# Second feed-forward sub-layer: VectorE transposes SwiGLU's result in 32x32 blocks instead of TensorE

## The chip, the cores and the metric

The kernel runs as one program on one core of a Trainium2 chip. The metric is the device time of one execution in microseconds (us): 1877.92 us, the median of three runs (1877.18 to 1877.95). The engines are named as in the profile: PE is TensorE (matmul), PEld its weight load, DVE is VectorE, ACT is ScalarE, POOL is GpSimd, and SP issues the transfers from HBM.

## What is computed

One decoder layer on 256 tokens of width 2048: a feed-forward sub-layer, a mixer, and a second feed-forward sub-layer (index 1). The change touches only the second feed-forward. Cut to what matters:

```
D_MODEL, SEQ, D_FF = 2048, 256, 5632

def swiglu(h, w_gate, w_up, w_down):
    return (jax.nn.silu(h @ w_gate) * (h @ w_up)) @ w_down

x = sublayer(x, 0, ffn(0), 0.5)
x = sublayer(x, 1, mixer, 1.0)
x = sublayer(x, 2, ffn(1), 0.5)     # sublayer: sandwich RMSNorm with adaLN shift, scale and gate
```

## The kernel before, in words

All data is float32. Each product is made of three matmuls in the fp32r type: a weight is split into a high part `wh` and a rest `wl`, the activations into `hh` and `hl`, and `mm3` (lines 308 to 311) adds high by high (L309), high activation by weight rest (L310) and activation rest by high weight (L311). The high part is a copy on ACT (L290, `wh`), the rest a subtraction on DVE (L291, `wl`).

Weights arrive as tiles `raw` of 128 x 1024 numbers (two blocks of 128 rows by 512 columns, 512 KB), in a ring of eight. Their split parts stand in rings of four buffers each (`NW = 4`, pool `wsp`). So the split of a tile waits until PE is done with the tile four places earlier. A tile takes twelve matmuls: two row blocks, two groups of 128 tokens, three products. Here "tile 0" is the first weight tile of a block's gate product.

The feed-forward's 5632 columns are taken in 11 blocks of 512. A block has eight tiles of the gate weights and eight of the up weights; both products stand in four PSUM banks with the tokens on the partitions (`proj_tok`). Then `swiglu_evac` takes the block out of PSUM: for each group `t` of 128 tokens ACT makes silu of the gate (L522) and DVE multiplies it with the up product (L523), which gives `gt`, 128 tokens x 512 columns. The product with `w_ff_down` wants the columns on the partitions, so `to_g` transposes each 128 x 128 piece on PE against an identity (L513: four into one PSUM bank, two banks a block), and `split_act` (L343 to L345) copies the high part of each bank into the slot `g` on ACT (L344) and subtracts on DVE (L345).

The blocks are taken in three groups of 4, 4 and 3. After a group the down product runs over four column quarters, with the same weight tiles and rings. A block's `g` is wanted only when the down product reaches its rows.

The order: `swiglu_evac` and `to_g` are generators in the list `pending`. After each weight tile's matmuls `pump` advances the first of them by one step, so a block's evacuation is issued among the first tiles of what comes next. A scheduler then orders each engine's instructions by its own costs; each engine runs its list strictly in order. A side job, `ada_unit`, works on the adaLN gate of the last sub-layer in between: DVE accumulates into `acc` from 16 transfers of `w_ada` (L168, L170), in a pool `adap` of two buffers with the tag `acc`, and `ada_row` finishes it (L200, L205 to L207).

Of the kernel before, what the change touches and what calls it, by code (L numbers as in the profile page):

```python
# [8 lines left out]
F32 = mybir.dt.float32  # L9
# [5 lines left out]
P = 128  # L15
D = 2048
S = 256
NT = S // P
# [14 lines left out]
def tile_layer(  # L33
# [6 lines left out]
    nc = tc.nc  # L40
    x, out, c = x[0], out[0], c[0]
# [15 lines left out]
    adap = ctx.enter_context(tc.tile_pool(name="adap", bufs=2))  # L57
# [7 lines left out]
    def nm(s):  # L65
        uid[0] += 1
        return f"{s}_{uid[0]}"

    def ps():
        return psp.tile([P, 512], F32, tag="ps", name=nm("ps"))  # L70

    def t2(shape=(P, 512), dtype=F32):
        return tp.tile(list(shape), dtype, tag="t2", name=nm("t2"))
# [178 lines left out]
    pending = []  # L252
# [17 lines left out]
    def flush():  # L270
        while pending:
            pump()
# [35 lines left out]
    def mm3(o, lh, ll, rh, rl, start, stop):  # L308
        nc.tensor.matmul(o, lh, rh, start=start, stop=False, skip_group_check=True)  # L309
        nc.tensor.matmul(o, lh, rl, start=False, stop=False, skip_group_check=True)  # L310
        nc.tensor.matmul(o, ll, rh, start=False, stop=stop, skip_group_check=True)  # L311
# [20 lines left out]
    def proj_tok(src, c0, begun=None, w=512, segs=FULL, banks=None, first=0):  # L332

        if begun is not None:
            banks, segs = begun[0], FULL[begun[1]:]
        banks = banks or [ps(), ps()]
        last = segs[-1][0] + segs[-1][1] - 1
        for k, wh, wl in w_tiles(src, segs, c0, w=w):
            for t in range(NT):
                tok_mm(k, wh, wl, t, banks[t][:, 0:w], first, last)  # L340
        return banks

    def split_act(dh, dl, src):  # L343
        act = nc.scalar.copy(dh, src)  # L344
        return nc.vector.tensor_tensor(out=dl, in0=src, in1=dh.bitcast(F32), op=ALU.subtract), act  # L345


    def parts():

        p = small((P, 8), "parts")  # L350
        nc.gpsimd.memset(p[:, 3:4], EPS)
        return p

    def sumsq(p, q, src):
        junk = t2()
        nc.scalar.activation(junk, src, AF.Square, scale=float(D) ** -0.5, accum_out=p[:, q + q // 3:q + q // 3 + 1])
# [81 lines left out]
    def early_w(src, c0, w):  # L438


        if src is None:
            return None
        tiles = []
        for half, h in enumerate((hh, hl)):
            raw = load_w(src, 2 * half, c0, w)
            v = h[:, 8:16, :].rearrange("p (a j u) s -> p a j (u s)", a=2, j=2)
            wh, wl = split_w(raw[:, :, 0:w], v, w)
            tiles += [(2 * half + j, wh[:, j, :], wl[:, j, :]) for j in range(2)]
        return tiles
# [54 lines left out]
        return banks, 2  # L504


    def to_g(g, gts):
        for i in range(2):
            pg = ps()
            for j in range(2):  # L510
                for t in range(NT):
                    m = 2 * i + j
                    nc.tensor.transpose(pg[:, j * S + t * P:j * S + (t + 1) * P], gts[t][:, m * P:(m + 1) * P], ident)  # L513
            split_act(g.t[:, 0, 2 * i:2 * i + 2, :], g.t[:, 1, 2 * i:2 * i + 2, :],
                      pg.rearrange("p (k s) -> p k s", s=S))
            yield

    def swiglu_evac(g, gb, ub):
        gts = []
        for t in range(NT):  # L520
            sg, gt = t2(), t2()
            nc.scalar.activation(sg, gb[t], AF.Silu)  # L522
            nc.vector.tensor_tensor(out=gt, in0=sg, in1=ub[t], op=ALU.mult)  # L523
            gts.append(gt)
        yield
        yield
        yield from to_g(g, gts)

    def swiglu_sum(gb, ub, part):

        pv = part.t.rearrange("p k s -> p (k s)")
        gts = []
        for t in range(NT):
            sg, gt = t2(), t2()
            nc.vector.tensor_tensor(out=sg, in0=pv[:, t * 512:(t + 1) * 512], in1=gb[t], op=ALU.add)
            nc.scalar.activation(sg, sg, AF.Silu)
            nc.vector.tensor_tensor(out=gt, in0=pv[:, 1024 + t * 512:1024 + (t + 1) * 512], in1=ub[t], op=ALU.add)
            nc.vector.tensor_tensor(out=gt, in0=sg, in1=gt, op=ALU.mult)
            gts.append(gt)
        part.free()  # L540
        g = Slot((P, 2, 4, S), F32R)

        def rest():
            yield
            yield
            yield from to_g(g, gts)

        pending.append(rest())
        return g

    def ffn(idx, supers, begun, xin, nxt, nxt_src=None, nxt_c0=None, nxt_w=512):

        y = None
        yp = [parts() for _ in range(NT)]

        def evac_y(si, q, t, bank):
            ys = y[t].t[:, q * 512:(q + 1) * 512]
            if si == 0:
                nc.scalar.copy(ys, bank)
            else:  # L560
                nc.vector.tensor_tensor(out=ys, in0=ys, in1=bank, op=ALU.add)
            if si == len(supers) - 1:
                sumsq(yp[t], q, ys)

        for si, blocks in enumerate(supers):
            gs = []
            n = len(blocks)
            for b, segs, part, banks in blocks:
                if si == 0 and begun is not None and not gs:
                    gb = proj_tok(w_ff_gate[idx], b * FB, begun)  # L570
                    ub = proj_tok(w_ff_up[idx], b * FB)
                elif part is not None:
                    gb = proj_tok(w_ff_gate[idx], b * FB, segs=segs, first=segs[0][0])
                    ub = proj_tok(w_ff_up[idx], b * FB, segs=segs, first=segs[0][0])
                    flush()
                    gs.append(swiglu_sum(gb, ub, part))
                    continue
                else:
                    gb = proj_tok(w_ff_gate[idx], b * FB, segs=segs, banks=banks and banks[0])
                    ub = proj_tok(w_ff_up[idx], b * FB, segs=segs, banks=banks and banks[1])  # L580
                flush()
                gs.append(Slot((P, 2, 4, S), F32R))
                pending.append(swiglu_evac(gs[-1], gb, ub))
            if y is None:
                y = [Slot((P, D)) for _ in range(NT)] if xin[0].__class__ is Half else [Half(t) for t in range(NT)]
            rows = [(4 * i, 4, 4 * b[0]) for i, b in enumerate(blocks)]

            def mms(k, wh, wl, t):
                g = gs[k // 4].t
                mm3(banks[t], g[:, 0, k % 4, t * P:(t + 1) * P], g[:, 1, k % 4, t * P:(t + 1) * P],  # L590
                    wh, wl, k == 0, k == 4 * n - 1)

            for q in range(4):
                banks = [ps(), ps()]
                if si == len(supers) - 1 and q == 2:
                    for s_ in xin:
                        s_.t
                if si == len(supers) - 1 and q == 3:
                    flush()
                    if side[0] is not None:  # L600
                        side[0].drain()
                    early = early_w(nxt_src, nxt_c0, nxt_w)
                    kept, slots = hold(w_ff_down[idx], rows, q * 512, NW if nxt is None else 3)

                    def last_mm(t):
                        for k, wh, wl in kept:
                            mms(k, wh, wl, t)

                    return boundary(last_mm, lambda t: evac_y(si, q, t, banks[t]), lambda t: times_gg(y, t, q), xin, y, yp, slots + gs,
                                    early, 1, nxt, nxt_src, nxt_c0, nxt_w)  # L610
                else:
                    for k, wh, wl in w_tiles(w_ff_down[idx], rows, q * 512):
                        for t in range(NT):
                            mms(k, wh, wl, t)
                    for t in range(NT):
                        later(evac_y, si, q, t, banks[t])
                        if si == len(supers) - 1:
                            later(times_gg, y, t, q)
            if si < len(supers) - 1:
                for g in gs:  # L620
                    g.free()
# [102 lines left out]

    blocks = [(4718, 410), (4308, 410), (3896, 412), (3484, 412), (G0, 412)]
    begun = ffn(0, supers, None, xin, 1, w_in, *blocks[0])
    side[0] = None

# [384 lines left out]
```

## Time and profile before

| what | value |
|---|---|
| median of three runs | 1877.92 us |
| the profiled execution, its own time | 1877.58 us |
| its span | 1875.9 us |
| PE busy | 1827.3 us, 97% |
| DVE busy | 1355.3 us, 72% |
| ACT busy | 853.4 us, 45% |
| TensorE clock, mean granted | 0.998 |

Busy times overlap between engines. The second feed-forward lies between about 1130 us and the end. A timeline row gives start, duration, engine, line, operation, output<-input and count; in brackets stands the idle time before it and what ended it. On one engine the start of the next instruction comes before the recorded end of the one ahead, since the records overlap a little; the distance from start to start is what an instruction costs in a row of them.

### The profile page before, as it was taken

To read this page: it belongs to the slowest core of one execution; us is meant where nothing else is said; L and a number is where in the kernel's file an instruction comes from. 1 tells how busy PE (TensorE), PEld (TensorE's weight loads), DVE (VectorE), ACT (ScalarE), POOL (GpSimd) and SP (SyncE) were. 2 spreads that over 40 slices of the span, in tenths; PEclk is the share of its full clock that TensorE was granted. 3 is DMA by queue.
4 is the path that set the end of the run, shared out by engine and by line. 5 is a ranking of instruction groups with operands and counts; after the bars stand their busy time and mean duration, and the time that the engine had idled before them with its cause. 6 is when DMAs were issued, how large, how long until landed. Compare 5 with 4: busy or idle time off the path is not lost.

```text
span 1875.9 us, 23017 instructions
## 1 busy us (share of the span) xinstructions
PE 1827.3 (97%) x8493; PEld 1530.3 (82%) x8493; DVE 1355.3 (72%) x1472; ACT 853.4 (45%) x1059; POOL 17.2 (1%) x40
## 2 busy tenths in 40 slices
PE   2999999999999999999999999999999999999998
PEld 2888888888888888799988887888888888888886
DVE  7788798788887878868898987555556555556555
ACT  3545444444443444555545446444444444334443
POOL 0000000000000000000000000000000000000000
PEclk9999999999999999999999999999999999999999
DMA  9999889999899999678789994776677776677652
GB/s 349 344 362 351 294 294 311 319 316 310 291 334 327 323 330 315 199 230 276 225 280 309 365 334 138 224 221 213 227 226 218 225 221 216 221 227 222 190 189 93
DMA packets 232618, 499.82 MB, mean 266 GB/s; under 512 B 16829, under 2 KB 28333, under 8 KB 231993
## 3 DMA queue, kind: packets, MB, share of 16 engines
q1 hardware_dynamic: 232504, 498.36, 79.9%
q8 instruction: 66, 1.08, 0.2%
q14 instruction: 48, 0.39, 0.1%
HBM read 496.19 MB, written 2.10 MB: 266 GB/s over the span
## 4 chain that ended last, share of the span: by engine, by line
PE 88%; issue 8%; DVE 2%; ACT 1%; POOL 1%; DMA 0%; SPq 0%; DVEq 0%; POOLq 0%; ACTq 0%
PE ps L309 29%; PE ps L311 28%; PE ps L310 28%; DVE acc L170 1%; PE ps L513 1%; PE ps L181 0%; DMA t<-in_g_pre_dram 0%; PE ps L411 0%; POOL rstd L362 0%; DVE wl L291 0%; ACT t L373 0%; PE ps L900 0%; POOL brs L778 0%; ACT hh L344 0%; PE ps L205 0%
## 5 line engine op out<-in xcount | busy, mean ns | idle before, releaser
L291 DVE TENSOR_TENSOR wl<-raw,wh 128x1024 fp32r<-128x1024 f32 (+2 forms) x637 | 768.6, 1210 | 457.5 <-ACT wh L290 456.9
L290 ACT CAST wh<-raw 128x1024 fp32r<-128x1024 f32 (+2 forms) x637 | 662.4, 1043 | 863.1 <-PE ps L311 737.5
L309 PE MATMUL ps<-wh,hh 128*128 128x512 f32 (+2 forms) x1680 | 651.6, 390 | 3.8 <-DVE t L386 2.4
L310 PE MATMUL ps<-wl,hh 128*128 128x512 f32 (+2 forms) x1680 | 648.6, 386 | 0.6 <-DVE wl L291 0.6
L311 PE MATMUL ps<-wh,hl 128*128 128x512 f32 (+2 forms) x1680 | 648.7, 386 | 0.0
L309 PEld LDWEIGHTS ps<-wh,hh 128*128 128x128 f32 x1680 | 315.8, 188 | 63.5 <-ACT hh L344 4.1
L310 PEld LDWEIGHTS ps<-wl,hh 128*128 128x128 f32 x1680 | 316.2, 188 | 61.2 <-DVE wl L291 2.6
L311 PEld LDWEIGHTS ps<-wh,hl 128*128 128x128 f32 x1680 | 315.6, 188 | 60.5
L170 DVE SCALAR_TENSOR_TENSOR acc<-raw,cs,acc 128x1024 f32<-128x1024 f32 x270 | 345.1, 1278 | 0.5
L309 PE MATMUL ps<-wh,big 128*128 128x512 f32 x804 | 315.4, 392 | 0.0
L311 PE MATMUL ps<-wh,big 128*128 128x512 f32 x804 | 313.2, 390 | 0.0
L310 PE MATMUL ps<-wl,big 128*128 128x512 f32 x804 | 312.8, 389 | 0.0
L311 PEld LDWEIGHTS ps<-wh,big 128*128 128x128 f32 x804 | 150.9, 188 | 31.9
L310 PEld LDWEIGHTS ps<-wl,big 128*128 128x128 f32 x804 | 151.0, 188 | 30.5
L309 PEld LDWEIGHTS ps<-wh,big 128*128 128x128 f32 x804 | 151.0, 188 | 30.5
L650 ACT COPY big<-ps 128x512 f32<-128x512 f32 x32 | 18.9, 589 | 44.2 <-PE ps L311 43.1
L309 PE MATMUL ps<-hh,wh 128*128 128x256 f32 x128 | 37.6, 294 | 0.0
L345 DVE TENSOR_TENSOR big<-ps,big 128x512 fp32r<-128x512 f32 x52 | 35.6, 684 | 1.2 <-ACT big L344 1.2
L311 PE MATMUL ps<-hh,wl 128*128 128x256 f32 x128 | 36.2, 283 | 0.0
L310 PE MATMUL ps<-hl,wh 128*128 128x256 f32 x128 | 36.2, 283 | 0.0
L181 PE MATMUL ps<-ident,acc 128*128 128x128 f32 x96 | 14.5, 285 | 18.6 <-DVE acc L170 18.6
L344 ACT CAST big<-ps 128x512 fp32r<-128x512 f32 x52 | 30.1, 578 | 0.0
(191 smaller groups left out, 756.9 us busy)
## 6 DMA issues: line engine op xcount, KB each, us to landing
raw<-in_w_ada_dram SPq DMA_DIRECT2D x224, 512.0 KB, 5.3
raw<-in_w_ff_gate_dram SPq DMA_DIRECT2D x176, 512.0 KB, 4.5
raw<-in_w_ff_up_dram SPq DMA_DIRECT2D x176, 512.0 KB, 4.6
raw<-in_w_ff_down_dram SPq DMA_DIRECT2D x176, 512.0 KB, 4.9
raw<-in_w_ada_dram SPq DMA_DIRECT2D x128, 256.0 KB, 5.4
raw<-in_w_in_dram SPq DMA_DIRECT2D x48, 512.0 KB, 5.0
raw<-in_w_out_dram SPq DMA_DIRECT2D x32, 512.0 KB, 7.0
raw<-in_w_in_dram SPq DMA_DIRECT2D x24, 412.0 KB, 4.4
```

The lines of the kernel that those rows point to most:

```text
L170: ins = nc.vector.scalar_tensor_tensor(a, raw[:, j, :, :], cs[:, k:k + 1], a, op0=ALU.mult, op1=ALU.add)
L181: nc.tensor.transpose(pa[:, i * P:(i + 1) * P], a[:, i * P:(i + 1) * P], ident)
L290: behind(nc.scalar.copy(wh, rawv), floor[1])
L291: last_split[0] = nc.vector.tensor_tensor(out=wl, in0=rawv, in1=wh.bitcast(F32), op=ALU.subtract)
L309: nc.tensor.matmul(o, lh, rh, start=start, stop=False, skip_group_check=True)
L310: nc.tensor.matmul(o, lh, rl, start=False, stop=False, skip_group_check=True)
L311: nc.tensor.matmul(o, ll, rh, start=False, stop=stop, skip_group_check=True)
L344: act = nc.scalar.copy(dh, src)
L345: return nc.vector.tensor_tensor(out=dl, in0=src, in1=dh.bitcast(F32), op=ALU.subtract), act
L513: nc.tensor.transpose(pg[:, j * S + t * P:j * S + (t + 1) * P], gts[t][:, m * P:(m + 1) * P], ident)
L650: nc.scalar.copy(part.t.rearrange("p k s -> p (k s)")[:, u * 1024 + i * 512:u * 1024 + (i + 1) * 512], banks[i])
```

## The change

In the second feed-forward (`idx == 1`) the generator `to_g_blocks` takes the place of `to_g`. A float32 buffer `gf` (128 x 4 x 256) comes from the pool `adap` with the tag `acc`. For each of the two groups of tokens, DVE issues 16 transposes: each reads 32 partitions of `gt` and four pieces of 32 columns, transposes the 32 x 32 blocks, and writes them to another (or the same) group of 32 partitions of `gf`. Then `split_act` runs twice, from `gf` in SBUF instead of from PSUM. The first feed-forward keeps `to_g`.

```diff
+    def to_g_blocks(g, gts):
+
+        gf = adap.tile([P, 4, S], F32, tag="acc", name=nm("gf"))
+        for t in range(NT):
+            g3 = gts[t].rearrange("p (m c) -> p m c", c=P)
+            for b in range(4):
+                for q in range(4):
+                    nc.vector.transpose(gf[q * 32:(q + 1) * 32, :, t * P + b * 32:t * P + (b + 1) * 32],
+                                        g3[b * 32:(b + 1) * 32, :, q * 32:(q + 1) * 32])
+            yield
+        for i in range(2):
+            split_act(g.t[:, 0, 2 * i:2 * i + 2, :], g.t[:, 1, 2 * i:2 * i + 2, :], gf[:, 2 * i:2 * i + 2, :])
+        yield
+
...
-    def swiglu_evac(g, gb, ub):
+    def swiglu_evac(g, gb, ub, blocks):
...
         yield
-        yield
-        yield from to_g(g, gts)
+        if blocks:
+            yield from to_g_blocks(g, gts)
+        else:
+            yield
+            yield from to_g(g, gts)
...
-                pending.append(swiglu_evac(gs[-1], gb, ub))
+                pending.append(swiglu_evac(gs[-1], gb, ub, idx == 1))
```

DVE's list at the third block of the second feed-forward, from the split of tile 1 on, before the change; `t` are the products of L523, `ps` PSUM banks, `big` the slot `g`:

```order
L291 TENSOR_TENSOR wl_10740<-raw_10737,wh_10739 128x1024
L291 TENSOR_TENSOR wl_10758<-raw_10755,wh_10757 128x1024
L523 TENSOR_TENSOR t_2128_10730<-t_2127_10729,ps_10556 128x512
L523 TENSOR_TENSOR t_2130_10734<-t_2129_10733,ps_10557 128x512
L291 TENSOR_TENSOR wl_10783<-raw_10780,wh_10782 128x1024
L291 TENSOR_TENSOR wl_10808<-raw_10805,wh_10807 128x1024
L291 TENSOR_TENSOR wl_10826<-raw_10823,wh_10825 128x1024
L170 SCALAR_TENSOR_TENSOR acc_9967<-raw_10706,cs,acc_9967 128x1024
L291 TENSOR_TENSOR wl_10847<-raw_10844,wh_10846 128x1024
L345 TENSOR_TENSOR big_10708<-ps_10773,big_10708 128x512
```

The same place in the changed kernel, where the multiplications are at L537:

```order
L291 TENSOR_TENSOR wl_10786<-raw_10783,wh_10785 128x1024
L291 TENSOR_TENSOR wl_10821<-raw_10818,wh_10820 128x1024
L537 TENSOR_TENSOR t_2126_10776<-t_2125_10775,ps_10602 128x512
L537 TENSOR_TENSOR t_2128_10780<-t_2127_10779,ps_10603 128x512
L514 STREAM_TRANSPOSE gf_10801<-t_2126_10776 32x4x32 x16
L514 STREAM_TRANSPOSE gf_10801<-t_2128_10780 32x4x32 x16
L291 TENSOR_TENSOR wl_10855<-raw_10852,wh_10854 128x1024
L345 TENSOR_TENSOR big_10754<-gf_10801,big_10754 128x512 x2
L291 TENSOR_TENSOR wl_10877<-raw_10874,wh_10876 128x1024
```

All 32 transposes of a block stand in one run between the multiplications and the subtraction for tile 3, and both L345 have moved up behind that subtraction. The second place is DVE's list at the fourth block, before:

```order
L291 TENSOR_TENSOR wl_11081<-raw_11078,wh_11080 128x1024
L523 TENSOR_TENSOR t_2191_11053<-t_2190_11052,ps_10880 128x512
L523 TENSOR_TENSOR t_2193_11057<-t_2192_11056,ps_10881 128x512
L170 SCALAR_TENSOR_TENSOR acc_9967<-raw_10973,cs,acc_9967 128x1024
L291 TENSOR_TENSOR wl_11109<-raw_11106,wh_11108 128x1024
L291 TENSOR_TENSOR wl_11134<-raw_11131,wh_11133 128x1024
```

And the fourth block in the changed kernel:

```order
L291 TENSOR_TENSOR wl_11167<-raw_11164,wh_11166 128x1024
L537 TENSOR_TENSOR t_2188_11122<-t_2187_11121,ps_10949 128x512
L537 TENSOR_TENSOR t_2190_11126<-t_2189_11125,ps_10950 128x512
L514 STREAM_TRANSPOSE gf_11147<-t_2188_11122 32x4x32 x16
L514 STREAM_TRANSPOSE gf_11147<-t_2190_11126 32x4x32 x16
L170 SCALAR_TENSOR_TENSOR acc_9967<-raw_11042,cs,acc_9967 128x1024
L291 TENSOR_TENSOR wl_11204<-raw_11201,wh_11203 128x1024
L345 TENSOR_TENSOR big_11098<-gf_11147,big_11098 128x512 x2
```

Here the accumulation L170 stands between the transposes and the subtraction for tile 3, as it stood between the multiplications and that subtraction before. The ninth block has the same order. The third place is ACT's list at the third block, from the second silu on, before:

```order
L522 ACTIVATE t_2129_10733<-ps_10386 128x512
L290 CAST wh_10782<-raw_10780 128x1024
L290 CAST wh_10807<-raw_10805 128x1024
L290 CAST wh_10825<-raw_10823 128x1024
L290 CAST wh_10846<-raw_10844 128x1024
L344 CAST big_10708<-ps_10773 128x512
L290 CAST wh_10864<-raw_10862 128x1024
L344 CAST big_10708<-ps_10798 128x512
```

And in the changed kernel, where silu is at L536:

```order
L536 ACTIVATE t_2127_10779<-ps_10409 128x512
L290 CAST wh_10854<-raw_10852 128x1024
L290 CAST wh_10876<-raw_10874 128x1024
L290 CAST wh_10894<-raw_10892 128x1024
L344 CAST big_10754<-gf_10801 128x512 x2
L290 CAST wh_10915<-raw_10913 128x1024
```

Both copies of `g` stand one tile earlier and together, ahead of the copy for tile 6. PE's list loses its 88 transposes in the second feed-forward, eight a block, and keeps the order of its matmuls. SP's list keeps its order but for one small transfer (L197) that moves by one place.

## Rows read from the trace of the kernel before

**Rows 1.** Page, part 1: busy time, share and instructions of TensorE.

```profile
PE 1827.3 (97%) x8493; PEld 1530.3 (82%) x8493; DVE 1355.3 (72%) x1472; ACT 853.4 (45%) x1059; POOL 17.2 (1%) x40
```

**Rows 2.** Page, part 4: the chain that ended last, by engine.

```profile
PE 88%; issue 8%; DVE 2%; ACT 1%; POOL 1%; DMA 0%; SPq 0%; DVEq 0%; POOLq 0%; ACTq 0%
```

**Rows 3.** Stretches: start:end, length, PE, PEld, DVE, ACT, POOL, clock, DMA.

```profile
1200.00:1300.00 100.00, 100.00 (x451) 82.76 (x450) 56.08 (x50) 42.67 (x45) 0.00 (x0) 1.00 0.69 216
1300.00:1400.00 100.00, 100.00 (x447) 82.78 (x446) 53.51 (x46) 43.61 (x46) 0.00 (x0) 1.00 0.71 225
```

**Rows 4.** Groups by line and shape, 1180 to 1800 us.

```profile
L291 DVE TENSOR_TENSOR wl<-raw,wh 128x1024 fp32r<-128x1024 f32 x224 | 274.3, 1225 | 270.2 <-ACT wh L290 270.2
...
L290 ACT CAST wh<-raw 128x1024 fp32r<-128x1024 f32 x224 | 236.2, 1054 | 342.9 <-PE ps L311 332.7 <-issue 7.3 <-DMA raw<-in_w_ff_gate_dram 2.1
...
L344 ACT CAST big<-ps 128x512 fp32r<-128x512 f32 x20 | 11.6, 579 | 0.0
```

**Rows 5.** Timeline of DVE, third block and the tiles before.

```profile
1251.30 1.22 DVE L291 TENSOR_TENSOR wl<-raw,wh 128x1024 fp32r<-128x1024 f32 x1 [1.50 <-ACT wh L290]
1254.02 1.23 DVE L291 TENSOR_TENSOR wl<-raw,wh 128x1024 fp32r<-128x1024 f32 x1 [1.50 <-ACT wh L290]
...
1267.62 1.23 DVE L291 TENSOR_TENSOR wl<-raw,wh 128x1024 fp32r<-128x1024 f32 x1 [1.50 <-ACT wh L290]
1268.77 1.28 DVE L523 TENSOR_TENSOR t<-t,ps 128x512 f32<-128x512 f32 x2
1270.34 1.23 DVE L291 TENSOR_TENSOR wl<-raw,wh 128x1024 fp32r<-128x1024 f32 x1 [0.30 <-ACT wh L290]
```

**Rows 6.** Timeline of PE, third block's transposes.

```profile
1277.22 0.60 PE L513 MATMUL ps<-ident,t 128*128 128x128 f32 x4
1277.57 0.48 PE L309 MATMUL ps<-wh,hh 128*128 128x512 f32 x1
...
1280.43 0.60 PE L513 MATMUL ps<-ident,t 128*128 128x128 f32 x4
```

**Rows 7.** Timeline of ACT, third block.

```profile
1269.25 1.05 ACT L290 CAST wh<-raw 128x1024 fp32r<-128x1024 f32 x1 [1.17 <-PE ps L311]
```

**Rows 8.** Timeline of DVE, fourth block.

```profile
1313.24 1.28 DVE L523 TENSOR_TENSOR t<-t,ps 128x512 f32<-128x512 f32 x2
1314.44 1.28 DVE L170 SCALAR_TENSOR_TENSOR acc<-raw,cs,acc 128x1024 f32<-128x1024 f32 x1
1315.64 1.22 DVE L291 TENSOR_TENSOR wl<-raw,wh 128x1024 fp32r<-128x1024 f32 x1
```

**Rows 9.** DVE's groups by line and shape, whole span: mean ns of one.

```profile
L523 DVE TENSOR_TENSOR t<-t,ps 128x512 f32<-128x512 f32 x28 | 18.0, 681 | 0.2 <-issue 0.2
...
L386 DVE TENSOR_SCALAR t<-xt,rstd 128x512 f32<-128x512 f32 x24 | 11.0, 481 | 3.8 <-POOL rstd L362 3.3 <-DMA raw<-in_w_ada_dram 0.4
...
L345 DVE TENSOR_TENSOR hl<-t,hh 128x256 fp32r<-128x256 f32 x20 | 7.8, 421 | 0.7 <-ACT hh L344 0.5
```

**Rows 10.** Timelines of DVE and PE, fifth block.

```profile
1445.72 1.29 DVE L207 SCALAR_TENSOR_TENSOR big<-ps,t 128x512 f32<-128x512 f32 x2 [0.83 <-PE ps L206]
1446.93 1.28 DVE L523 TENSOR_TENSOR t<-t,ps 128x512 f32<-128x512 f32 x2
1448.12 1.22 DVE L291 TENSOR_TENSOR wl<-raw,wh 128x1024 fp32r<-128x1024 f32 x1
...
1454.16 0.60 PE L513 MATMUL ps<-ident,t 128*128 128x128 f32 x4
```

**Rows 11.** Timeline of DVE: short instructions in a row.

```profile
37.57 1.43 DVE L345 TENSOR_TENSOR hl<-t,hh 128x256 fp32r<-128x256 f32 x4
...
924.77 1.12 DVE L905 SCALAR_TENSOR_TENSOR big<-ps,v,big 128x128 f32<-128x128 f32 x4
925.80 1.21 DVE L291 TENSOR_TENSOR wl<-raw,wh 128x1024 fp32r<-128x1024 f32 x1
...
1128.58 0.88 DVE L386 TENSOR_SCALAR t<-xt,rstd 128x512 f32<-128x512 f32 x2 [0.67 <-POOL rstd L362]
```

## The prediction, made before the changed kernel ran

> **What bounds the kernel now.** I read the busy times first: PE works 97% of the span [rows 1]. Then the chain of waits that ended last: 88% of it is PE, 2% DVE [rows 2]. Then the stretches of the second feed-forward: PE is busy in all of each 100 us, DVE in 54 to 56 us [rows 3]. So a microsecond of PE work that goes here is a microsecond of the kernel, and DVE has free time on average. An average doesn't say whether it is free where 32 transposes stand in a row, so the groups by line come next: DVE's subtractions wait for ACT's copies, 270.2 us in all, and those copies wait for PE, 332.7 us [rows 4]. Both run as far ahead as the ring of four lets them and then wait for PE to hand back a buffer. The question is how far ahead that is when the transposes come.
>
> The timelines answer it. Tiles follow each other every 2.72 us (1254.02 - 1251.30), twelve matmuls of 0.227 us [rows 5]. At the third block the transposes stand after tile 2, at 1277.22 [rows 6], so tile 0 began three tiles earlier, at 1269.06. The multiplications start at 1268.77 [rows 5], 0.29 us before that, because DVE has by then split tiles 0, 1 and 2. Next on DVE is the subtraction for tile 3, whose copy on ACT started at 1269.25, when PE gave back the buffer [rows 7].
>
> **What goes.** Eight transposes a block, in two runs of four. From the start of one run to the start of the next pass 3.21 us (1280.43 - 1277.22) [rows 6], against 2.72 for a tile alone: 0.49 a run, 0.98 a block. Another reading: from one block's multiplications to the next pass 44.47 us (1313.24 - 1268.77) [rows 5, 8], against 16 x 2.72 = 43.52: 0.95 a block. I take 0.95; 11 blocks give **10.5 us** less on PE, all of it on the path while PE never waits.
>
> **What comes.** 32 transposes a block on DVE, 352 in all, each of 32 partitions x 128 elements, in one run. Let T be the time from the start of one to the start of the next. Two multiplications take 0.60 us each from start to start (1.28 for two, less 0.68 for one) [rows 5, 9], so the run starts at 1268.77 + 1.20 = 1269.97. Behind it stands the subtraction for tile 3, 1.23 us [rows 5], and a hand-over that I put at 0.04, since the copy of 1269.25 lasts 1.05 and the subtraction follows at 1270.34 [rows 5, 7]. PE wants its result for the second matmul of tile 3, at 1277.22 + 0.23 = 1277.45, now that no transposes stand there. That leaves 1277.45 - 1269.97 - 1.23 - 0.04 = **6.2 us** for the run: 0.194 us for one. What is over delays PE.
>
> Eight blocks are so. In the fourth and the ninth an accumulation follows the transposes, at 1.20 us from start to start (1315.64 - 1314.44) [rows 8]: 5.0 us are left. In the fifth, two instructions for the adaLN row hold back the multiplications to 1446.93, and PE wants tile 3 at 1454.16 + 0.23 [rows 10]: 1454.39 - 1446.93 - 1.20 - 1.22 - 0.04 = 5.0 too. So the wait is 8 x (32T - 6.2) + 3 x (32T - 5.0), and with the gain the change in us is **352T - 64.6 - 10.5 = 352T - 75.1**, for T over 0.194. It is even at T = 0.213.
>
> **T.** No transpose on DVE is in the trace, so I bound it. From below: a subtraction of 512 elements costs 0.60, one of 256 costs 0.337 (four in 1.43, one lasts 0.421: 1.01 / 3) [rows 9, 11]; that is 1.03 ns an element and 0.07 fixed, so 128 elements at one a cycle cost 0.205. A form with one source that goes faster per element doesn't end lower: two L386 of 512 take 0.88, one 0.481, so 0.40 from start to start [rows 9, 11]; taking off 384 elements at half of 1.03 ns leaves 0.20. From above: 0.337, if each element takes two steps. The only run of instructions with just 128 elements is L905: four in 1.03 us (925.80 - 924.77), 0.258 each [rows 11], an operation with a column of scalars.
>
> I take **0.238**: 0.205, and 32 more elements (0.033) because a transposed row isn't known before the last of the 32 columns is in, and I assume that the next instruction doesn't use that time. It lies between the lower bound and L905's. Then 32T = 7.62; eight blocks wait 1.42, three 2.62: 11.4 + 7.9 = 19.3, less 10.5: **+8.8 us**. The profiled execution took 1877.6 us, 0.3 under the median; the sum goes from it: 1886.4 us.
>
> [...]
>
> **What I cost at nothing.** L345 twice, moved up behind the subtraction for tile 3: 1.2 us and then 1.2 for tile 4's subtraction, within the 2.72 us in which PE works on tile 3. Without that cover it would be up to 0.7 us a block. L345's wait for ACT's copies: two of 0.58 us [rows 4] run during the subtraction for tile 3. ACT's copy for tile 6 is queued behind them and ends about 11 us after tile 0's start; PE wants tile 6 after 16. The transfers: `raw` is given back up to 7 us later, but the ring has eight, so the next use of a buffer is eight tiles, 22 us, away. `gf` shares the two buffers of `acc`; a new one is wanted 44 us after the last, when its readers are long done. The last `g` of the third group is ready about 11 us after tile 0's start; the down product reaches it at its tile 4, 10.9 us and the wait later, so it just holds.
>
> **The rivals.** First, *the array's filling is hidden* under the instruction ahead, and a transpose costs what any stream of 128 elements costs: T = 0.205, 32T = 6.56. Eight blocks wait 0.36, three 1.56: 7.6 - 10.5 = -2.9, **1874.7 us**. This is the side of not slower; it decides from T = 0.213 down. For it: subtractions follow each other with only 0.07 us of fixed cost, so DVE hides most of an instruction's latency [rows 9, 11]. Against it: the only measured run of 128 elements is dearer, 0.258. At 0.203 it begins to be a gain that can be told from none.
>
> Second, *a transpose doesn't run at one element a cycle*, because of four-byte elements or because each of the four 32 x 32 blocks fills and empties by itself: T = 0.337, 32T = 10.8. Waits of 4.6 and 5.8 us: 36.6 + 17.3 - 10.5 = +43.4, **1921.0 us**. DVE would then be busy some 70% of the stretch, so an average would not show it. For it speaks only that nothing in the trace excludes it; in between lies T = 0.258, with +15.8 us, 1893.4.
>
> Third, that the run is hidden anyway, since DVE is idle 1.5 us of every 2.72 [rows 5]. It would need T under 0.16 for all blocks (-10.5, 1867.1), under the lower bound; I give it 3%.
>
> **How the numbers follow.** Forecast (T from 0.224 to 0.27): 0.44. First rival (0.203 to 0.224 and somewhat below): 0.34. Second (over 0.27): 0.19. Third: 0.03. A change under 0.2%, 3.8 us, can't be told from none here; by the formula that is T from 0.203 to 0.224. Faster: the third and the lower part of the first, 0.13. Same: 0.24. Slower: 0.63. The range goes from 1873 (T = 0.20, the lower bound) to 1904 (T = 0.289, over L905's): some 6% lie below and 13% above. The forecast's own range is 1881 to 1898.
>
> **What would show it.** Right: L514 in runs of 16 with starts 0.23 to 0.25 us apart; PE idle before L310 of tile 3, released by L291, 11 times, 1.4 us in most blocks and 2.6 in three; from one block's multiplications to the next 43.5 + 1.4 us instead of 44.47. First rival: starts 0.205 apart and waits of 0.4. Second: 0.30 and more, PE idle over 40 us in all. The forecast is wrong in kind if PE waits for something else: ACT's copies for L309, `g` in the down product, or a transfer.

## The result, and the profile after

| | before | changed |
|---|---|---|
| median | 1877.84 us (1877.18 to 1877.95, 4 runs) | 1934.9 us (1934.64 to 1936.1, 4 runs) |
| ratio, 95% interval | | 1.0305 (1.0292 to 1.0318) |
| span of the profiled execution | 1875.9 us | 1933.1 us |
| mean granted clock | 0.998 | 0.984 |

The change costs 57.1 us where 8.8 were forecast. The page of the changed kernel, parts 1, 4 and 5 (against [rows 1, 2]):

```profile
PE 1841.7 (95%) x8405; PEld 1537.3 (80%) x8405; DVE 1458.3 (75%) x1824; ACT 854.6 (44%) x1059; POOL 17.2 (1%) x40
...
PE 80%; DVE 9%; issue 8%; ACT 1%; DMA 1%; POOL 1%; SPq 0%; POOLq 0%; DVEq 0%; ACTq 0%
...
L514 DVE STREAM_TRANSPOSE gf<-t 32x128 f32<-32x128 f32 x352 | 106.5, 303 | 4.7
```

DVE is on the chain with 9% instead of 2%, yet busy only 75% of the span: the average still looks harmless. PE issues 88 instructions less and is busy 14 us longer, which already says that it ran slower somewhere. The timeline of DVE at the first, second and third blocks (against [rows 5]):

```profile
1180.29 1.28 DVE L537 TENSOR_TENSOR t<-t,ps 128x512 f32<-128x512 f32 x2
...
1229.25 1.28 DVE L537 TENSOR_TENSOR t<-t,ps 128x512 f32<-128x512 f32 x2
...
1241.73 1.29 DVE L345 TENSOR_TENSOR big<-gf,big 128x512 fp32r<-128x512 f32 x2
1242.93 1.28 DVE L170 SCALAR_TENSOR_TENSOR acc<-raw,cs,acc 128x1024 f32<-128x1024 f32 x1
1244.13 4.71 DVE L291 TENSOR_TENSOR wl<-raw,wh 128x1024 fp32r<-128x1024 f32 x4
...
1279.51 1.28 DVE L537 TENSOR_TENSOR t<-t,ps 128x512 f32<-128x512 f32 x2
1280.70 10.11 DVE L514 STREAM_TRANSPOSE gf<-t 32x128 f32<-32x128 f32 x32
1290.85 1.23 DVE L291 TENSOR_TENSOR wl<-raw,wh 128x1024 fp32r<-128x1024 f32 x1
```

From the first transpose to the subtraction behind the last pass 10.15 us (1290.85 - 1280.70), 0.317 each. One lasts 0.303, so none overlaps the next; all other instructions in [rows 9, 11] did, by some 0.08 (L523 lasts 0.68 and costs 0.60 from start to start). The timeline of PE at the third block, and the stretches of 4 us around it (start:end, length, PE, PEld, DVE, ACT, POOL, clock, DMA):

```profile
1287.73 0.39 PE L311 MATMUL ps<-wh,hl 128*128 128x512 f32 x1
1287.96 0.61 PE L309 MATMUL ps<-wh,hh 128*128 128x512 f32 x2
1292.12 0.56 PE L310 MATMUL ps<-wl,hh 128*128 128x512 f32 x1 [3.55 <-DVE wl L291]
1292.48 0.63 PE L311 MATMUL ps<-wh,hl 128*128 128x512 f32 x1
1292.91 0.63 PE L310 MATMUL ps<-wl,hh 128*128 128x512 f32 x1
...
1295.88 0.39 PE L311 MATMUL ps<-wh,hl 128*128 128x512 f32 x1
1296.11 0.39 PE L309 MATMUL ps<-wh,hh 128*128 128x512 f32 x1
```

```profile
1284.00:1288.00 4.00, 4.00 (x20) 3.30 (x19) 3.82 (x14) 1.05 (x1) 0.00 (x0) 1.00 0.02 4
1288.00:1292.00 4.00, 0.57 (x3) 0.15 (x1) 3.86 (x11) 1.15 (x3) 0.00 (x0) 1.00 0.00 0
1292.00:1296.00 4.00, 3.88 (x10) 3.07 (x11) 4.00 (x6) 0.93 (x1) 0.00 (x0) 0.57 0.57 146
1296.00:1300.00 4.00, 4.00 (x19) 3.26 (x18) 3.01 (x3) 1.95 (x2) 0.00 (x0) 1.00 0.93 331
```

Two losses stand here. PE waits before L310 of tile 3 for DVE's subtraction, as the prediction said: tile 3 begins at 1287.96 with two matmuls of L309, the third would have come at 1288.41 and came at 1292.12, 3.71 us late (4.9 in the fourth, fifth and ninth blocks). And behind the wait the granted clock is 0.57 for a stretch (0.50 from 1293 to 1295): matmuls start 0.43 apart instead of 0.227, and from 1292.12 to 1295.88 nine of them take 3.76 us instead of 2.04. Together that is 5.43 us, and tile 3 takes 8.15 us (1296.11 - 1287.96) instead of 2.72. The prediction had no word on the clock.

In the kernel before, L310 was the second matmul of tile 3, and only one L309 (1277.57, [rows 6]) stood ahead of it:

```profile
1277.89 0.40 PE L310 MATMUL ps<-wl,hh 128*128 128x512 f32 x1
```

So PE's list doesn't keep the order of its matmuls, as the part on the change says it does: in tile 3 a second L309 was moved ahead of L310, and the wait is 0.23 us shorter for it.

The slow stretch is not equally long in each block. In the second it reaches into tile 4:

```profile
1241.87 0.79 PE L310 MATMUL ps<-wl,hh 128*128 128x512 f32 x1 [3.55 <-DVE wl L291]
...
1246.30 1.06 PE L309 MATMUL ps<-wh,hh 128*128 128x512 f32 x2
1247.15 0.63 PE L310 MATMUL ps<-wl,hh 128*128 128x512 f32 x1
...
1248.27 0.39 PE L311 MATMUL ps<-wh,hl 128*128 128x512 f32 x1
```

From 1241.87 to 1248.27 fifteen matmuls take 6.40 us instead of 3.40. That is why the second block takes 50.26 us to the next (1279.51 - 1229.25) and the first 48.96 (1229.25 - 1180.29). Added up in this way from PE's timeline, the matmuls behind the eleven waits take 1.4 to 3.0 us too long, 22.5 us in all.

### The profile page after: what moved, and what is told of

It is laid out like the page before. It is cut to its first block, busy times and chain, and to the rows that moved or that the text cites. A ratio compares the mean times of both kernels' runs of the same rounds, so it can differ in the third digit from the quotient of the medians.

```text
span 1933.1 us, 23216 instructions
## 1 busy us (share of the span) xinstructions
PE 1841.7 (95%) x8405; PEld 1537.3 (80%) x8405; DVE 1458.3 (75%) x1824; ACT 854.6 (44%) x1059; POOL 17.2 (1%) x40
## 4 chain that ended last, share of the span: by engine, by line
PE 80%; DVE 9%; issue 8%; ACT 1%; DMA 1%; POOL 1%; SPq 0%; POOLq 0%; DVEq 0%; ACTq 0%
PE ps L310 26%; PE ps L311 26%; PE ps L309 26%; DVE gf L514 5%; DVE wl L291 2%; DVE acc L170 1%; ACT wh L290 1%; DVE t L537 1%; PE ps L527 0%; PE ps L181 0%; DMA t<-in_g_pre_dram 0%; PE ps L411 0%; POOL rstd L362 0%; ACT t L373 0%; DMA raw<-in_w_in_dram 0%
## 5 line engine op out<-in xcount | busy, mean ns | idle before, releaser
L310 PE MATMUL ps<-wl,hh 128*128 128x512 f32 (+2 forms) x1680 | 657.5, 391 | 31.5 <-DVE wl L291 31.5
L309 PE MATMUL ps<-wh,hh 128*128 128x512 f32 (+2 forms) x1680 | 654.0, 392 | 3.8 <-ACT hh L344 3.2
L311 PE MATMUL ps<-wh,hl 128*128 128x512 f32 (+2 forms) x1680 | 655.6, 390 | 0.0
L310 PEld LDWEIGHTS ps<-wl,hh 128*128 128x128 f32 x1680 | 320.6, 191 | 96.9 <-DVE wl L291 36.7
L309 PEld LDWEIGHTS ps<-wh,hh 128*128 128x128 f32 x1680 | 319.2, 190 | 65.2 <-ACT hh L344 4.2
L311 PEld LDWEIGHTS ps<-wh,hl 128*128 128x128 f32 x1680 | 320.3, 191 | 61.4
L170 DVE SCALAR_TENSOR_TENSOR acc<-raw,cs,acc 128x1024 f32<-128x1024 f32 x270 | 345.3, 1279 | 0.6
L310 PE MATMUL ps<-wl,big 128*128 128x512 f32 x804 | 316.1, 393 | 11.8 <-DVE wl L291 11.8
L309 PE MATMUL ps<-wh,big 128*128 128x512 f32 x804 | 315.9, 394 | 0.0
L311 PE MATMUL ps<-wh,big 128*128 128x512 f32 x804 | 315.7, 393 | 0.0
L310 PEld LDWEIGHTS ps<-wl,big 128*128 128x128 f32 x804 | 152.7, 190 | 44.4 <-DVE wl L291 13.4
L311 PEld LDWEIGHTS ps<-wh,big 128*128 128x128 f32 x804 | 152.4, 190 | 32.0
L309 PEld LDWEIGHTS ps<-wh,big 128*128 128x128 f32 x804 | 152.1, 189 | 31.1
L514 DVE STREAM_TRANSPOSE gf<-t 32x128 f32<-32x128 f32 x352 | 106.5, 303 | 4.7
L309 PE MATMUL ps<-hh,wh 128*128 128x256 f32 x128 | 37.6, 294 | 0.0
L311 PE MATMUL ps<-hh,wl 128*128 128x256 f32 x128 | 36.2, 283 | 0.0
L310 PE MATMUL ps<-hl,wh 128*128 128x256 f32 x128 | 36.2, 283 | 0.0
L344 ACT CAST big<-gf 128x512 fp32r<-128x512 f32 x22 | 12.5, 616 | 46.4 <-DVE gf L514 46.4
```

The source lines that it names most:

```text
L170: ins = nc.vector.scalar_tensor_tensor(a, raw[:, j, :, :], cs[:, k:k + 1], a, op0=ALU.mult, op1=ALU.add)
L514: nc.vector.transpose(gf[q * 32:(q + 1) * 32, :, t * P + b * 32:t * P + (b + 1) * 32], g3[b * 32:(b + 1) * 32, :, q * 32:(q + 1) * 32])
```

## The experiments

Theories on T after the result: **D**, a transpose on DVE always holds the engine to its end; **L**, instructions on 32 partitions do; **G**, the sending to another group of partitions costs. On the rest of the loss: **C**, PE's wait costs twice, itself and the slow clock behind it.

**Eight transposes over 128 partitions.**

```diff
-                for q in range(4):
-                    nc.vector.transpose(gf[q * 32:(q + 1) * 32, :, t * P + b * 32:t * P + (b + 1) * 32],
-                                        g3[b * 32:(b + 1) * 32, :, q * 32:(q + 1) * 32])
+                nc.vector.transpose(gf[:, :, t * P + b * 32:t * P + (b + 1) * 32],
+                                    g3[:, :, b * 32:(b + 1) * 32])
```

> Eight transposes a block instead of 32, each over all 128 partitions; each 32x32 block stays in its group of partitions, so the blocks are not sent to other groups and the result is not the layer's. Theory D (a transpose on DVE holds the engine to its end, whatever its lanes): starts 0.317 us apart as in the changed kernel, 8 x 0.317 = 2.5 us, under the 6.2 us of room, so PE never waits and only the 10.5 us of its own transposes go: 1867.3 us, clock 0.998. Theory L (only instructions on 32 partitions are so slow): starts 0.20 to 0.24 apart, and the same 1867.3 us. Both say that the whole loss is the length of the run.

Measured: 1867.66 us, ratio 0.9946 (0.9929 to 0.9963), clock 0.999. DVE's timeline in this kernel:

```profile
1268.38 1.66 DVE L513 STREAM_TRANSPOSE gf<-t 128x128 f32<-128x128 f32 x8
1269.96 1.18 DVE L291 TENSOR_TENSOR wl<-raw,wh 128x1024 fp32r<-128x1024 f32 x1
```

Eight start in 1.58 us, 0.198 each, though each lasts 0.27. So a transpose as such costs no more than the prediction worked out for a plain stream of 128 elements (0.205), and it overlaps its neighbours; D falls. The gain on PE's side is confirmed: 9.9 us less than the kernel before in the same series (1877.57), against 10.5.

**32 copies instead of transposes.**

```diff
-                    nc.vector.transpose(gf[q * 32:(q + 1) * 32, :, t * P + b * 32:t * P + (b + 1) * 32],
+                    nc.vector.tensor_copy(gf[q * 32:(q + 1) * 32, :, t * P + b * 32:t * P + (b + 1) * 32],
```

> The 32 transposes of a block are 32 plain copies with the same slices, 32 partitions to another group of 32; the 32x32 blocks are moved but not transposed, so the result is not the layer's. Theory D (it is the transpose): starts about 0.205 apart, run 6.6 us, waits of 0.4 us in eight blocks and 1.6 in three: 1875 us, or a few us more if short waits too lower the clock. Theory G or L (it is the sending to another group, or 32 partitions): starts 0.317 apart and 1934.9 us, as the changed kernel.

Measured: 1889.64 us, ratio 1.0062 (1.0047 to 1.0077): between the two. DVE's group and its timeline at the third block:

```profile
L514 DVE COPY gf<-t 32x128 f32<-32x128 f32 x352 | 76.9, 218 | 4.5
```

```profile
1271.74 7.41 DVE L514 COPY gf<-t 32x128 f32<-32x128 f32 x32
1279.18 1.23 DVE L291 TENSOR_TENSOR wl<-raw,wh 128x1024 fp32r<-128x1024 f32 x1
```

0.2325 from start to start at 0.218 each: the copies don't overlap either, they are only shorter. No run has copies that keep their group, so what the change of group adds to a copy is not shown. It isn't the transposing. L or G stands.

**32 transposes that stay in their group.**

```diff
-                    nc.vector.transpose(gf[q * 32:(q + 1) * 32, :, t * P + b * 32:t * P + (b + 1) * 32],
+                    nc.vector.transpose(gf[b * 32:(b + 1) * 32, :, t * P + q * 32:t * P + (q + 1) * 32],
```

> 32 transposes of 32 partitions a block, but each writes to the group of partitions that it reads, so nothing is sent to another group and the result is not the layer's. Theory D or L: starts 0.317 apart, 1934.9 us as the changed kernel. Theory G (the sending costs): starts 0.20 to 0.24 apart, 1875 to 1887 us.

Measured: 1882.72 us, ratio 1.0027 (1.0016 to 1.0039). DVE's timeline:

```profile
1270.98 7.17 DVE L514 STREAM_TRANSPOSE gf<-t 32x128 f32<-32x128 f32 x32
1278.18 1.22 DVE L291 TENSOR_TENSOR wl<-raw,wh 128x1024 fp32r<-128x1024 f32 x1
```

0.225 on average, with 32 partitions: L falls, and G seems right. But in this kernel the group also changes only with each fourth instruction, so two readings of G were left: the sending within an instruction (S), or the change from one instruction to the next, of the output's group (W) or the input's (R).

**26 transposes, two of them over 128 partitions.**

```diff
-            for b in range(4):
+            for b in range(3):
...
+            nc.vector.transpose(gf[:, :, t * P + 96:t * P + 128], g3[:, :, 96:128])
```

> 26 transposes a block instead of 32: of each token group's four pieces the fourth is one transpose over 128 partitions that stays in its groups, so a quarter of the blocks is not sent and the result is not the layer's. With 0.317 us each the run is 8.24 us, and PE waits 2.0 us in eight blocks and 3.2 in three: 26.0 less 10.5 is +15.5, 1893.3 us, if the clock stays. If every wait of PE costs the clock about 1.9 us a block as in the changed kernel: 1914 us. If only the waits over 3 us do: 1899.

Measured: 1895.64 us, ratio 1.0093 (1.0078 to 1.0108). PE and clock at the third block:

```profile
1281.18 0.50 PE L310 MATMUL ps<-wl,hh 128*128 128x512 f32 x1 [1.59 <-DVE wl L291]
1281.51 0.39 PE L311 MATMUL ps<-wh,hl 128*128 128x512 f32 x1
```

```profile
1280.00:1284.00 4.00, 2.82 (x12) 2.36 (x13) 4.00 (x6) 2.09 (x3) 0.00 (x0) 1.00 0.41 117
```

A wait of 1.59 us, the size that the prediction had reckoned with, leaves the clock at 1.00. The time lies between the sum without any clock loss (1893.3) and the one with it in the long waits alone (1899). Here the prediction's sum (15.5 for this run) is nearly right: 18.1. In the profiled execution, the fastest of the four (1893.39 us), the clock fell behind one of the three long waits (2.59 us) and not behind the two of 2.56.

**The inner loops exchanged.**

```diff
-            for b in range(4):
-                for q in range(4):
+            for q in range(4):
+                for b in range(4):
```

> The changed kernel with the two inner loops exchanged: four transposes in a row write to the same group of partitions and read from four groups; the result is the layer's. Theory W (a new group of the output costs about 0.12 us): three of four starts 0.20 apart, run 7.2 us as where each block stayed in its group, about 1883 us. Theory R (a new group of the input costs it): 0.317 apart throughout, 1935 us. Theory S (an instruction whose output lies in another group than its input costs it): 12 of 16 dear, about 0.29 apart, 1922 us.

Measured: 1934.42 us, ratio 1.0302 (1.0288 to 1.0316); DVE's timeline:

```profile
1277.70 10.11 DVE L514 STREAM_TRANSPOSE gf<-t 32x128 f32<-32x128 f32 x32
```

Four outputs in a row in the same group don't help when the input's group changes: 0.317 again, as in the changed kernel, where the input's group stays for four and the output's changes. So neither W nor R alone; a change of either is enough, or S.

**Own groups, another one each time.** The kernel of the third experiment with the two inner loops exchanged as above.

> 32 transposes that stay in their own group of partitions, as in the run before, but in an order in which input and output go to a new group with each instruction; nothing is sent, so the result is not the layer's. Theory W or R (the change of group from one instruction to the next costs): 0.317 apart, 1935 us. Theory S (only sending costs): 0.20 to 0.225 apart, 1876 to 1883 us.

Measured: 1933.72 us, ratio 1.0297 (1.0283 to 1.0311):

```profile
1278.98 10.10 DVE L514 STREAM_TRANSPOSE gf<-t 32x128 f32<-32x128 f32 x32
```

Nothing is sent here, and it is as dear. S falls: what costs is that an instruction uses another group of 32 partitions than the one ahead of it.

**Pairs.**

```diff
-        for t in range(NT):
-            g3 = gts[t].rearrange("p (m c) -> p m c", c=P)
-            for b in range(4):
-                for q in range(4):
-                    nc.vector.transpose(gf[q * 32:(q + 1) * 32, :, t * P + b * 32:t * P + (b + 1) * 32],
-                                        g3[b * 32:(b + 1) * 32, :, q * 32:(q + 1) * 32])
-            yield
+        g3 = [gt.rearrange("p (m c) -> p m c", c=P) for gt in gts]
+        yield
+        for b in range(4):
+            for q in range(4):
+                for t in range(NT):
+                    nc.vector.transpose(gf[q * 32:(q + 1) * 32, :, t * P + b * 32:t * P + (b + 1) * 32],
+                                        g3[t][b * 32:(b + 1) * 32, :, q * 32:(q + 1) * 32])
+        yield
```

> The changed kernel with the loop over the two token groups innermost: each two transposes in a row have the same group of partitions as input and the same as output, then both may change; still one run of 32, and the result is the layer's. If a change of either group costs 0.12 us and nothing else does: starts 0.317 and 0.20 apart in turn, run 16 x 0.517 = 8.3 us, waits of 2.1 us in eight blocks and 3.3 in three, less 10.5: +16 us, 1894 us, the clock kept. If an instruction that sends to another group is always dear: 1935 us.

Measured: 1897.93 us, ratio 1.0106 (1.0092 to 1.012). DVE's timeline at the third block, and PE's rows and stretches at the third and ninth:

```profile
1273.11 8.14 DVE L515 STREAM_TRANSPOSE gf<-t 32x128 f32<-32x128 f32 x32
1281.28 1.23 DVE L291 TENSOR_TENSOR wl<-raw,wh 128x1024 fp32r<-128x1024 f32 x1
```

```profile
1282.56 0.50 PE L310 MATMUL ps<-wl,hh 128*128 128x512 f32 x1 [1.58 <-DVE wl L291]
...
1737.55 0.50 PE L310 MATMUL ps<-wl,hh 128*128 128x512 f32 x1 [2.78 <-DVE wl L291]
```

```profile
1284.00:1288.00 4.00, 4.00 (x20) 3.27 (x19) 4.00 (x4) 1.09 (x2) 0.00 (x0) 1.00 0.78 251
...
1738.00:1742.00 4.00, 4.00 (x13) 3.12 (x11) 3.56 (x5) 0.61 (x1) 0.00 (x0) 0.57 0.85 281
```

The run takes 8.17 us, 0.511 a pair, where 0.517 was expected (0.317 and 0.194 make 0.511), though every transpose sends to where the changed kernel does. The time is 4 us over the expected 1894, and the clock is not kept everywhere: behind the wait of 1.58 us it is 1.00, behind those of 2.8 us in the fourth, fifth and ninth blocks it falls (0.57 here).

**PE kept busy during its wait.**

```diff
+            if t == 1:
+                pd = ps()
+                for _ in range(15):
+                    nc.tensor.matmul(pd, hh[:, 0, 0:P], hh[:, 0:2, :].rearrange("p k s -> p (k s)"), start=True, stop=True)
             yield
```

> The changed kernel with 15 more matmuls of 512 columns a block, which nobody reads, on PE just ahead of tile 3, where it waits 3.9 us; they take 15 x 0.227 = 3.4 us of that wait; the result is the layer's. Theory C (the wait costs twice: itself, and the half clock behind it): 1.5 to 1.9 us a block come back, 1914 to 1918 us, granted clock 1.00 behind tile 3. Without it: 1935 us, since the work that DVE has to do stays the same.

Measured: 1917.45 us, ratio 1.0211 (1.0197 to 1.0225). PE's timeline at the second and the third block, and the stretches behind the third's wait:

```profile
1243.77 0.50 PE L310 MATMUL ps<-wl,hh 128*128 128x512 f32 x1 [0.48 <-DVE wl L291]
...
1284.48 3.56 PE L519 MATMUL ps<-hh 128*128 128x512 f32 x15
...
1288.64 0.50 PE L310 MATMUL ps<-wl,hh 128*128 128x512 f32 x1 [0.37 <-DVE wl L291]
```

```profile
1288.00:1292.00 4.00, 3.63 (x17) 2.75 (x16) 4.00 (x6) 1.94 (x3) 0.00 (x0) 1.00 0.42 132
1292.00:1296.00 4.00, 4.00 (x19) 3.34 (x18) 4.00 (x5) 1.61 (x2) 0.00 (x0) 1.00 0.92 291
```

With 165 matmuls more the kernel is 17.5 us faster than the changed one. DVE's run is the same, and so is the time at which it hands over; the clock behind the wait is 1.00 instead of 0.57. C holds. Its price is more than the 17.5 us won, since two things are dearer here. Only one L309 stands ahead of L310 again, so the fill (3.40 us) and the wait behind it delay PE by 3.93 us (1288.64 - 1284.48, less 0.23 for L309) where the wait alone did by 3.71: 2.4 us over 11 blocks. And in the second and seventh blocks PE, at the full clock, comes to L310 of tile 4 before DVE's subtraction is done (the row at 1243.77), 0.64 us each. With these 3.7 us the slow clock cost 21.2 us in the changed kernel. The rows agree: of the 22.5 us behind the waits 0.11 a wait is there at the full clock too (L311 starts 0.33 behind L310 in the run with 26), which leaves 21.3, some 1.9 a block.

How long PE has to wait for the clock to fall can't be read from these runs. In the kernel with own groups it fell at the fourth block, whose tile 3 belongs to the down product, behind 1.80 us, and in the one with the loops exchanged it stayed in the first block behind 3.54:

```profile
1325.07 0.59 PE L310 MATMUL ps<-wl,big 128*128 128x512 f32 x1 [1.80 <-DVE wl L291]
...
1324.00:1328.00 4.00, 2.93 (x7) 2.30 (x8) 4.00 (x5) 0.68 (x1) 0.00 (x0) 0.67 0.69 211
```

```profile
1191.73 0.50 PE L310 MATMUL ps<-wl,hh 128*128 128x512 f32 x1 [3.54 <-DVE wl L291]
...
1192.00:1196.00 4.00, 4.00 (x19) 3.23 (x19) 4.00 (x5) 1.59 (x2) 0.00 (x0) 1.00 0.65 162
```

**The transposes spread.**

```diff
-            for b in range(4):
-                for q in range(4):
-                    nc.vector.transpose(gf[q * 32:(q + 1) * 32, :, t * P + b * 32:t * P + (b + 1) * 32],
-                                        g3[b * 32:(b + 1) * 32, :, q * 32:(q + 1) * 32])
-            yield
+            for b in range(4):
+                for q in range(4):
+                    behind(nc.vector.transpose(gf[q * 32:(q + 1) * 32, :, t * P + b * 32:t * P + (b + 1) * 32],
+                                               g3[b * 32:(b + 1) * 32, :, q * 32:(q + 1) * 32]), last_split[0])
+                yield
...
-                pending.append(swiglu_evac(gs[-1], gb, ub, idx == 1))
+                pending.append(swiglu_evac(gs[-1], gb, ub, idx == 1 and len(gs) < n))
```

> The transposes of a block are put in steps of four, one step behind each weight tile's subtraction, and the last block of each group of blocks keeps TensorE's transposes; the result is the layer's. If the length of the run is the cause: four take 1.27 us and fit into the 1.5 us that DVE idles at each tile, PE never waits, and eight blocks save 0.95 us each: 1870.0 us, clock 0.999. If DVE's work itself costs PE time, wherever it stands: 1900 us or more.

Measured: 1869.94 us, ratio 0.9959 (0.9946 to 0.9973). DVE's timeline at the third block, and the stretch with the second and third:

```profile
1269.12 2.50 DVE L514 STREAM_TRANSPOSE gf<-t 32x128 f32<-32x128 f32 x8
1271.65 1.23 DVE L291 TENSOR_TENSOR wl<-raw,wh 128x1024 fp32r<-128x1024 f32 x1
1272.91 1.25 DVE L514 STREAM_TRANSPOSE gf<-t 32x128 f32<-32x128 f32 x4
```

```profile
1200.00:1300.00 100.00, 100.00 (x443) 82.81 (x442) 78.62 (x121) 44.28 (x48) 0.00 (x0) 1.00 0.74 225
```

The same 32 transposes at the same 0.316 each ((1271.65 - 1269.12) / 8; the first two steps of a block come together), and DVE busier than before the change (78.6 us of 100 against 56.1, [rows 3]), yet PE never waits. It is the length of the run alone that cost, not DVE's work.

**Pairs, spread.** The pairs with `behind(..., last_split[0])`, four transposes a step, eight a step in the last block of the first two groups; the last block of all keeps PE's transposes.

```diff
+        for i in range(16):
+            b, q = i // 4, i % 4
+            for t in range(NT):
+                behind(nc.vector.transpose(gf[q * 32:(q + 1) * 32, :, t * P + b * 32:t * P + (b + 1) * 32],
+                                           g3[t][b * 32:(b + 1) * 32, :, q * 32:(q + 1) * 32]), last_split[0])
+            if (i + 1) % step == 0:
+                yield
...
+                pending.append(swiglu_evac(gs[-1], gb, ub, 0 if idx == 0 else 2 if len(gs) < n else 4 if n == 4 else 0))
```

> The pairs, spread: four transposes behind each weight tile's subtraction, eight in the last block of the first two groups of blocks; only the very last block keeps TensorE's transposes; the result is the layer's. Ten blocks save 0.95 us each and PE doesn't wait: 1868.5 us, 1.5 less than with four a step and eight blocks. If eight at a tile are too many: 1870 or more.

Measured: 1868.8 us, ratio 0.9952 (0.9938 to 0.9966), where 1868.5 was expected. It beats both kernels, by 9.1 and 66.1 us. That it is better than the version with fours (1869.94) can't be told from these intervals.

## Why the prediction was wrong

- **The bound and the gain** were right: without a wait, 9.9 us go (10.5 predicted).
- **The place** was right, and **the room** nearly: PE waits at L310 of tile 3 for DVE's subtraction. With T = 0.317 the room of 6.2 us gives 10.15 - 6.2 = 3.95 us; the rows show 3.71. The prediction took L310 for the second matmul of the tile, and in the changed list it is the third.
- **T is the term that was mis-sized**: 0.238 forecast, 0.317 measured, outside the forecast's 0.27. I built it from instructions on all 128 partitions and added 0.033, my estimate for the time until a transposed row is known. No run shows that term: over 128 partitions the next transpose starts 0.198 behind the one ahead, under my lower bound of 0.20. What I had not priced is that each instruction goes to another group of partitions than the one ahead and then doesn't overlap it: 0.12 each. By the prediction's own formula T = 0.317 gives +36.5 us instead of +8.8; with the second L309 ahead of L310 it is 2.5 us less.
- **A step was missing**: "what is over delays PE" was priced at the length of the wait. Behind waits of 3.55 to 4.77 us PE's clock falls, which costs 21.3 us over the 11 blocks. Behind the eight waits of 1.4 us that I forecast this term would have been nothing, as the run with 26 shows for 1.59; behind the three of 2.6 the clock can fall, as it did there behind one of three, for 1.6 us. The wrong T brought most of it in.
- **An edit costed at nothing**: L345 moved up, behind it L170 in the second and seventh blocks, so that tile 4's subtraction comes later. I had checked the order of the third block and not of these two. At the full clock this delays PE by 0.64 us in each of the two, as the kernel with the filled wait shows. In the changed kernel it costs nothing: PE is slow there, and L310 of tile 4 (1247.15) has no idle time before it.
- **The sum**: the waits delay PE by 8 x 3.71 + 3 x 4.92 = 44.4 us, the matmuls behind them take 22.5 us too long, and 9.9 us go: 57.0 of 57.1 us. Why the slow stretch lasts longer in some blocks than in others stays open.
- **The rivals**: the second had the size of T nearly (over 0.27) and the wrong cause: a transpose by itself costs 0.198, not two steps an element. The first, a plain stream (0.205), is nearly what the transposes cost where they stay on the same partitions (0.194 to 0.198).

With a steady change of groups, sending (10.11 us a run) and not sending (10.10) cost the same. What cost was the change from one instruction to the next: 0.317 against 0.198. A float32 transpose over 128 partitions lasts 0.269 (median), and one over 32 partitions in the changed kernel 0.303. These are durations; what counted was whether they overlap.

## What to carry to other kernels

Where a transformed piece moves from a saturated engine to one with idle time, compare the longest run of the new instructions with the time by which the feeding engine is ahead, not with its average idle time; spread in pieces of four, the same work cost nothing here. Price a wait of the matmul engine twice when it is a few microseconds long: itself, and the clock behind it (1.3 to 2.9 us a wait here, behind waits of 3.55 to 4.77 us). And take the price of many small instructions from rows that do what they do, changes of partitions included, or measure it by itself first.

## What the runs showed of the hardware

- On DVE a transpose on another group of 32 partitions than the one ahead, for input or output, doesn't overlap it: 0.317 us from start to start instead of 0.194 to 0.198, for 128 elements. Copies that change their group don't overlap either (0.2325, each lasting 0.218).
- A float32 transpose of 128 elements a partition takes 0.198 from start to start over 128 partitions, no more than the 0.205 estimated for a plain stream from the rows of longer instructions.
- In the second feed-forward of the profiled executions the granted clock stayed at 1.00 behind all of PE's waits for DVE's subtraction of up to 1.59 us. It fell behind two of three waits of 1.8 us, two of three of 2.3, one of three of 2.6, all three of 2.8, and 31 of 33 of 3.5 to 4.8 us. Matmuls that nobody reads, put into the wait, kept it up and made the kernel faster.
